# First adaLN scale by column halves with the first products between them, shift on TensorE, and 12 instead of 17 weight blocks split ahead, in a two-layer decoder trunk

## The chip, the cores and the metric

The kernel runs on one core of one Trainium2 chip. The metric is device time in microseconds (us) of one execution. The time before is 1517.57 us, the median of 3 runs (1512.85 to 1518.46). All rows below come from one profiled execution of it, which took 1515.52 us, with a span of 1513.8 us from the first to the last instruction.

Engines are written as the profile writes them: PE is TensorE, PEld its weight loads, DVE VectorE, ACT ScalarE, POOL GpSimd, SP SyncE, which issues most of the transfers.

## The reference

One sequence of 512 tokens of width 1024 goes through two layers. Each sub-layer is an RMS norm, an adaLN scale and shift computed from a condition vector `c`, a mixer, a gate and a residual add.

```
def ada_modulation(c, w, b):
    mod = jax.nn.silu(c) @ w + b
    return jnp.split(mod[:, None, :], 6, axis=-1)
...
    h = rms_norm(x, norm_mix) * (1 + sc_m) + sh_m
    fq, fk, fv, fgl, sq, sk, sv = _split(h @ w_in, EVEN_SPLITS)
...
    mix = jnp.concatenate([o_fox.reshape(B, S, -1), o_swa.reshape(B, S, -1)], axis=-1) @ w_out
    x = x + g_m * mix
    h = rms_norm(x, norm_ffn) * (1 + sc_f) + sh_f
    return x + g_f * swiglu(h, ffn_gate, ffn_up, ffn_down)
```

Layer 0 mixes with forgetting attention on half of the heads and sliding-window attention on the other half, then a dense SwiGLU of width 2816. Layer 1 mixes with sparse attention (an indexer picks 128 keys per query), then a top-2-of-8 expert SwiGLU and a final norm. Everything is float32 in and out.

## The kernel before

Activations stand transposed, features on the 128 partitions in 8 k-tiles (`KT`) of 512 tokens. A float32 product is made as three products of a high and a low half (`mm3`): weights high by activations high, high by low, low by high. The high half of a weight block is an ACT cast (`wh`), the low half a DVE subtraction (`wl`); raw blocks of 512 KB come over the SP queue into a pool of three buffers each (`weights(3, 3, 3)`). `norm` and the first stage make activations `h[k]` of the same two halves.

The work of one engine runs in one fixed order. A scheduler writes that order out when the program is built, by the order of the code and its own estimates; `tc.issue_after(x)` puts an instruction behind `x` in it. On the chip each engine takes its instructions strictly in this order and waits on semaphores.

The start works as follows. The norm sums (`ssqt`) are 16 small PE products; their root gives `rstd`, which PE spreads over the partitions, and DVE makes `xn[k]`, eight normed tiles without scale. Meanwhile `ada(0, 1, ...)` computes the first scale on PE: eight loads of 512 KB of `eada`, sixteen products with 32 output columns, four of which stand beside each other in the array at `tile_position` 0, 32, 64 and 96. Its sum is turned by four transposes (`ada_t`) and becomes `a` (name `A00`, in rows `A`). Then come `h[k]` of scale alone, and `NEARLY` = 3 first products of 24 matmuls each (`first`), on weight blocks that were split early (`early`). The shift is not in them yet: `ada_vector(0, (0,), ...)` computes it on DVE with 16 multiply-adds (`acc<-side`) and four PE products that sum over partitions (`ones`). It is added to the three finished products as a bias (`L844`, `L845`, `L850`), and to `h[k]` for all later products (`L859`, `L860`). The memory of this stage (`st_`) is reused by the attention stage (`at`), so the first instruction that writes there (`kd`, L608) waits until the last shifted `h[k]` is made.

In the dense SwiGLU PE makes gate and up products (`pj`) in two groups of 12 and 10 column blocks, each followed by `down` (`dn`). Beside them `ada_vector` computes later scales and shifts on DVE; its loads (`side`, two buffers) are issued by POOL when DVE has used up a buffer. The last of these chains is for the two vectors (1, (4, 5)). Also beside them, `split_ahead` prepares the input projection of layer 1 (`oin`, 17 blocks): load a block (`araw`), cast it (L316), subtract on DVE (L318), store the low half to DRAM (`olow`). Its steps are taken one in each of the eight steps of each `down`, and one in every second step of the second gate and up group. Layer 1 then loads raw and low halves of all 17 blocks (`wload`, L331).

In layer 1 POOL makes the two rope multiplications of each projection (`rope`, L568 and L569) while DVE picks keys (`choose`, MAX and MATCH_REPLACE); ACT casts the roped queries (`qs`), which the first scores (`ss`, L643) need.

## Time and profile before

| what | value |
|---|---|
| median of 3 runs | 1517.57 us |
| the profiled execution | 1515.52 us |
| its span | 1513.8 us |
| mean granted clock of PE | 0.979 |
| PE busy share of the span | 95% |
| DVE busy share | 68% |
| ACT busy share | 50% |
| POOL busy share | 9% |

The granted clock is 1.0 where PE has its full 2.4 GHz and 0.5 where it has 1.2 GHz. An idle time is noted in square brackets behind an instruction, with the instruction or transfer that ended it. Times are counted from the span's start.

### The profile page before, as it was taken

What the parts mean: (1) busy time and instruction counts of PE and PEld (TensorE: products, weight loads), DVE (VectorE), ACT (ScalarE), POOL (GpSimd) and SP (SyncE); (2) the same over time, 40 slices, a digit from 0 to 9 for tenths busy, and PEclk for the clock granted to TensorE, in tenths of its full rate; (3) what the DMA queues carried; (4) which work ended last, traced back from release to release, by engine and by line L of the source; (5) the groups of instructions that cost most, each with busy time, mean ns of one, the idle gap of its engine ahead of it and who ended that gap; (6) DMA issues with size and microseconds to landing.
All of it is one profiled execution on the core that took longest, in us unless ns stands there. A gap on an engine that the chain in (4) does not pass through costs nothing.

```text
span 1513.8 us, 23866 instructions
## 1 busy us (share of the span) xinstructions
PE 1431.5 (95%) x8683; PEld 1079.4 (71%) x8683; DVE 1033.3 (68%) x1909; ACT 750.6 (50%) x1257; POOL 129.9 (9%) x158
## 2 busy tenths in 40 slices
PE   5999999899999999898989999999999999999994
PEld 2766777678787878686767577776767777787773
DVE  5845587766665446644789753876767896897784
ACT  4554473332222332334436752755556675675672
POOL 1000000011010001001132100101010100100000
PEclk9999999899999999998999999999999999999997
DMA  8445325466688547644554102767787998897791
GB/s 315 141 128 148 82 83 191 170 209 210 196 261 292 169 130 260 230 148 123 169 156 127 48 29 86 301 220 243 254 267 250 319 342 262 276 377 247 268 388 60
DMA packets 91951, 309.32 MB, mean 204 GB/s; under 512 B 11304, under 2 KB 12088, under 8 KB 91824
## 3 DMA queue, kind: packets, MB, share of 16 engines
q1 hardware_dynamic: 77952, 259.93, 50.7%
q0 software_dynamic: 13872, 47.78, 10.3%
q8 instruction: 70, 1.15, 0.3%
q14 instruction: 57, 0.47, 0.1%
HBM read 278.64 MB, written 19.97 MB: 197 GB/s over the span
## 4 chain that ended last, share of the span: by engine, by line
PE 47%; DVE 5%; DMA 2%; ACT 2%; issue 1%; POOL 1%; SPq 0%; DVEq 0%; ACTq 0%; POOLq 0%
PE v L1370 4%; PE g L1363 3%; PE u L1364 3%; PE u L1363 3%; PE g L1365 3%; PE u L1365 3%; PE g L1364 3%; PE dn L336 2%; PE dn L338 2%; PE dn L337 2%; PE yv L1370 2%; PE yg L1363 2%; PE o L714 2%; PE ss L643 2%; PE yu L1363 1%; PE yu L1364 1%
## 5 line engine op out<-in xcount | busy, mean ns | idle before, releaser
L298 ACT CAST wh<-raw 128x1024 fp32r<-128x1024 f32 (+2 forms) x387 | 381.6, 992 | 406.8 <-PE dn L337 90.6
L299 DVE TENSOR_TENSOR wl<-raw,wh 128x1024 fp32r<-128x1024 f32 (+2 forms) x387 | 441.9, 1153 | 150.1 <-ACT wh L298 145.2
L336 PE MATMUL pj<-h,wh 128*128 128x512 f32 x560 | 226.1, 406 | 5.3 <-ACT h L486 3.2
L338 PE MATMUL pj<-h,wl 128*128 128x512 f32 (+1 forms) x560 | 225.0, 403 | 1.7 <-DVE wl L299 1.7
L337 PE MATMUL pj<-h,wh 128*128 128x512 f32 (+1 forms) x560 | 223.9, 401 | 0.1
L406 DVE SCALAR_TENSOR_TENSOR acc<-side,sc,acc 128x512 f32<-128x512 f32 x140 | 103.5, 750 | 52.9 <-DMA side<-in_oada 47.0
L336 PEld LDWEIGHTS pj<-h,wh 128*128 128x128 f32 x560 | 106.2, 190 | 36.7 <-ACT h L486 4.0
L338 PEld LDWEIGHTS pj<-h,wl 128*128 128x128 f32 (+1 forms) x560 | 106.4, 190 | 28.8 <-DVE wl L299 2.1
L337 PEld LDWEIGHTS pj<-h,wh 128*128 128x128 f32 (+1 forms) x560 | 105.9, 189 | 27.2 <-issue 2.2
L1363 PE MATMUL g<-wh,xe 128*128 128x512 f32 (+1 forms) x192 | 79.3, 413 | 1.2 <-ACT xe L1355 1.2
L338 PE MATMUL dn<-hid,wl 128*128 128x512 f32 x176 | 71.5, 406 | 2.3 <-DVE wl L299 2.3
L1363 PE MATMUL u<-wh,xe 128*128 128x512 f32 (+1 forms) x192 | 72.8, 379 | 0.0
L1364 PE MATMUL u<-wl,xe 128*128 128x512 f32 (+1 forms) x192 | 72.7, 378 | 0.0
L1365 PE MATMUL g<-wh,xe 128*128 128x512 f32 (+1 forms) x192 | 72.4, 377 | 0.0
L1364 PE MATMUL g<-wl,xe 128*128 128x512 f32 (+1 forms) x192 | 72.2, 376 | 0.0
L1365 PE MATMUL u<-wh,xe 128*128 128x512 f32 (+1 forms) x192 | 72.1, 376 | 0.0
L336 PE MATMUL dn<-hid,wh 128*128 128x512 f32 x176 | 71.3, 405 | 0.0
L337 PE MATMUL dn<-hid,wh 128*128 128x512 f32 x176 | 70.5, 401 | 0.0
L1370 PE MATMUL v<-raw,xf 128*32 128x128 f32 x1760 | 67.3, 276 | 0.0
L690 ACT ACTIVATE p<-p,st 128x128 f32<-128x128 f32 (+3 forms) x96 | 53.6, 560 | 25.0 <-DVE st L687 24.5
L1370 PEld LDWEIGHTS v<-raw,xf 128*32 128x32 f32 x1760 | 49.3, 109 | 21.4 <-issue 12.2
L526 DVE SCALAR_TENSOR_TENSOR xT<-dn,mod,xT 128x512 f32<-128x512 f32 x32 | 24.0, 750 | 53.1 <-PE dn L338 53.1
(419 smaller groups left out, 2661.2 us busy)
## 6 DMA issues: line engine op xcount, KB each, us to landing
raw<-in_xgu SPq DMA_DIRECT2D x128, 512.0 KB
raw<-in_xdn SPq DMA_DIRECT2D x88, 512.0 KB
side<-in_oada POOLq DMA_DIRECT2D x48, 512.0 KB, 4.7
raw<-in_xgu SPq DMA_DIRECT2D x64, 384.0 KB
raw<-in_egu SPq DMA_DIRECT2D x44, 512.0 KB
side<-in_eada SPq DMA_DIRECT2D x24, 512.0 KB
araw<-in_oin SPq DMA_DIRECT2D x16, 512.0 KB
olow<-araw SPq DMA_DIRECT2D x16, 512.0 KB
```

The source lines that it names most:

```text
L298: stream["cast"] = A.copy(wh[:, :n], raw[:, :n]).ins
L299: stream["sub"] = V.tensor_sub(wl[:, :n], raw[:, :n], wh[:, :n].bitcast(F32)).ins
L336: T.matmul(out_, wh, xh, start=start, stop=False)
L337: T.matmul(out_, wh, xl, start=False, stop=False)
L338: T.matmul(out_, wl, xh, start=False, stop=stop)
L406: V.scalar_tensor_tensor(s, r, sc[:, k:k + 1], s, op0=ALU.mult, op1=ALU.add)
L643: T.matmul(b[:, j, :nk], qs[p, a, t * P:(t + 1) * P], k[p, c, :nk], start=a == c, stop=a == 1, tile_position=(64 * j, 0))
L690: A.activation(ps_[j][:, :nk], ps_[j][:, :nk], AF.Exp, bias=st[:, j:j + 1], scale=-1.0, accum_out=rc[:, i, j:j + 1])
L1363: T.matmul(o, x[0], wh, start=first, stop=False)
L1364: T.matmul(o, x[0], wl, start=False, stop=False)
L1365: T.matmul(o, x[1], wh, start=False, stop=last)
L1370: T.matmul(o[32 * j:32 * j + 32], x[2], w[:, j * width:(j + 1) * width], start=first, stop=last, tile_position=(0, 32 * j), skip_group_che ...
```

## The change

There are two independent parts.

The first is the start. The scale is computed in two halves of its columns (`scale(0)`, `scale(1)`): each half has four loads and eight products, two rounds of four beside each other in the array. The loads of the first half go ahead of the early weight blocks. After the first half of the scale, k-tiles 0 to 3 of `h` are made, and the first four k-tiles of products 0 and 1; then the second half of the scale, the first four k-tiles of product 2, and the last four k-tiles of all three. The shift is no longer computed on DVE: `ada(0, 0, ...)` makes it with sixteen products, eight behind product 0 and eight behind product 1. The loads of later weight blocks are kept behind the loads of this stage (`pin`).

The second part is `AHEAD = 12`: only 12 of the 17 blocks of `oin` are split ahead, and only in the steps of `down`. The other five are split when they are used, with the subtraction on POOL.

```
+AHEAD = 12
...
-        self.ap, self.at, self.low = ap, 0, None
+        self.ap, self.at, self.low, self.left = ap, 0, None, 0
...
-        stream["load"] = nc.sync.dma_start(raw[:, :n], src).ins
+        with tc.issue_after(stream["pin"]) if stream.get("pin") else ExitStack():
+            stream["load"] = nc.sync.dma_start(raw[:, :n], src).ins
...
-        stream["sub"] = V.tensor_sub(wl[:, :n], raw[:, :n], wh[:, :n].bitcast(F32)).ins
+        stream["sub"] = (G if blocks.low else V).tensor_sub(wl[:, :n], raw[:, :n], wh[:, :n].bitcast(F32)).ins
...
     def wload(blocks, nk, ncol):
-        if blocks.low is not None:
+        if blocks.low and blocks.left:
+            blocks.left -= 1
...
+            def scale(g, after=None):
+                raws = [load(src(g, kp), 1024) for kp in range(4)]
+                yield
+                pt = bank("pt", "ada")
+                with tc.issue_after(after) if after else ExitStack():
+                    for k in range(KT):
+                        q = 32 * (k % 4)
+                        T.matmul(pt[q:q + 32, :], cb[:, k], raws[k // 2][:, k % 2 * 512:k % 2 * 512 + 512], start=k < 4,
+                                 stop=k > 3, tile_position=(0, q))
+                rows_ = t512("ada_row")
+                A.copy(rows_, pt)
+                pc = aux("ada_t")
+                for n in range(4):
+                    T.transpose(pc[:, n * P:(n + 1) * P], rows_[:, n * P:(n + 1) * P], identf)
+                part = t512("ada_s")[:, :4]
+                V.tensor_reduce(part, pc.rearrange("p (n h r) -> p n h r", n=4, r=32)[:, :, :, 0], axis=AX.X, op=ALU.add)
+                c = slice(4 * g, 4 * g + 4)
...
+                for k in range(4 * g, 4 * g + 4):
+                    hk = hp.tile([P, 2, S], F32R, name=f"h{k}", tag=f"h{k}")
+                    A.activation(hk[:, 0], xn[k], AF.Copy, scale=a[:, k:k + 1])
+                    V.scalar_tensor_tensor(hk[:, 1], xn[k], a[:, k:k + 1], hk[:, 0].bitcast(F32), op0=ALU.mult, op1=ALU.subtract)
+                    h.append(hk)
+                yield
...
-            fill(ada(0, 1, load, "pt"), 99)
...
+            fill(scale(0), 2)
+            for i in range(NEARLY):
+                early(i)
+            begin(0, range(4))
+            second = scale(1, begin(1, range(4)))
+            fill(second, 1)
+            shift = ada(0, 0, load, "mm")
+            fill(second, 1)
+            begin(2, range(4))
             for i in range(NEARLY):
-                if i == SHIFT:
-                    fill(ada_vector(0, (0,), st_, nc.sync, NS0), 99)
...
+                ins = begin(i, range(4, KT))
+                if i < NEARLY - 1:
+                    with tc.issue_after(ins):
+                        fill(shift, 2)
+            stream["pin"] = stream["early"]
+            fill(shift, 1)
...
-                            [KT * n if n <= P else KT // 2 * n for n in O_IN for _ in range(1 if n <= P else 2)])
+                            [KT * n if n <= P else KT // 2 * n for n in O_IN for _ in range(1 if n <= P else 2)][:AHEAD])
...
-                if grp == FFN_GROUPS[-1] and c % 2:
-                    fill(ahead)
...
-            oin.low = Blocks(olow)
+            oin.low, oin.left = Blocks(olow), AHEAD
```

`begin(i, ks)` makes product `i` for the k-tiles `ks` with `mm3`.

The order of the instructions shows three places. The first is PE at the very start, before and then of the changed kernel; `ada` are the products of the scale, `ssqt` the norm sums, `rstd` the spreading of the root, `first` the first products.

```order
L461 MATMUL ssqt<-ones_102,ssqa 128x1 x4
L461 MATMUL ssqt<-ones_102,sq 128x1 x4
L382 MATMUL ada<-st,cb 32x512
L475 MATMUL rstd<-identf,rs_r 128x128 x4
L382 MATMUL ada<-st,cb 32x512 x15
L360 MATMUL ada_t<-identf,ada_row 128x128 x4
L336 MATMUL first<-h_253,early_193 128x512 x3
```

```order
L828 MATMUL ada<-st,cb 32x512
L464 MATMUL ssqt<-ones_102,ssqa 128x1 x4
L464 MATMUL ssqt<-ones_102,sq 128x1 x4
L828 MATMUL ada<-st,cb 32x512 x7
L478 MATMUL rstd<-identf,rs_r 128x128 x4
L834 MATMUL ada_t<-identf,ada_row 128x128 x4
L339 MATMUL first<-h_224,early_193 128x512 x2
```

Before, one of the sixteen products of the scale stood ahead of `rstd`; now all eight of the first half do, one of them ahead of the norm sums.

On DVE at the same place, `xn` are the normed tiles, `early` the low halves of the three early weight blocks, `A` the scale; the rows run from the root to the first low halves of `h`, without the first seven of the eight `xn`.

```order
L812 TENSOR_TENSOR early_194<-st,early_193 128x8x128
L796 TENSOR_TENSOR xn_191<-xT,rstd 128x512
L369 TENSOR_REDUCE ada_s<-ada_t 128x8
L370 TENSOR_TENSOR mod_243<-ada_s,vec 128x8
L819 SCALAR_TENSOR_TENSOR A_251<-mod_243,vec 128x8
L812 TENSOR_TENSOR early_194<-st,early_193 128x8x128
L824 SCALAR_TENSOR_TENSOR h_253<-xn_177,A_251,h_253 128x512
```

```order
L799 TENSOR_TENSOR xn_191<-xT,rstd 128x512
L836 TENSOR_REDUCE ada_s<-ada_t 128x4
L815 TENSOR_TENSOR early_194<-st,early_193 128x8x128
L838 TENSOR_TENSOR ada_s<-ada_s,vec 128x4
L815 TENSOR_TENSOR early_194<-st,early_193 128x8x128
L839 SCALAR_TENSOR_TENSOR A_195<-ada_s,vec 128x4
L815 TENSOR_TENSOR early_194<-st,early_193 128x8x128
L843 SCALAR_TENSOR_TENSOR h_224<-xn_177,A_195,h_224 128x512
```

The scale still stands behind all eight `xn`, and two of the three subtractions for the early blocks, which stood ahead of `xn`, now stand between the reduction and the scale.

The second place is DVE in the second gate and up group, in the chain of (1, (4, 5)): `acc` are its multiply-adds, `araw` is the subtraction of the split ahead, `sg` and `hid` belong to the gate.

```order
L404 TENSOR_SCALAR acc<-side,sc 128x512
L406 SCALAR_TENSOR_TENSOR acc<-side,sc,acc 128x512 x3
L299 TENSOR_TENSOR wl<-raw,wh 128x1024
L406 SCALAR_TENSOR_TENSOR acc<-side,sc,acc 128x512
L318 TENSOR_TENSOR araw<-araw,awh 128x1024
L406 SCALAR_TENSOR_TENSOR acc<-side,sc,acc 128x512 x3
L973 TENSOR_TENSOR sg<-pj,sg 128x512
```

```order
L407 TENSOR_SCALAR acc<-side,sc 128x512
L409 SCALAR_TENSOR_TENSOR acc<-side,sc,acc 128x512 x3
L301 TENSOR_TENSOR wl<-raw,wh 128x1024
L409 SCALAR_TENSOR_TENSOR acc<-side,sc,acc 128x512 x4
L1010 TENSOR_TENSOR sg<-pj,sg 128x512
```

The subtraction is gone from between the multiply-adds, at two places of this chain; the order of the rest is the same there.

The third place is POOL in the sparse attention: pairs of rope multiplications, and in the changed kernel the subtractions of the late blocks (`wl`).

```order
L568 TENSOR_TENSOR rq<-rq,cosT 128x512
L569 TENSOR_TENSOR rr<-rr,sinT 128x512
L568 TENSOR_TENSOR rq<-rq,cosT 128x512
L569 TENSOR_TENSOR rr<-rr,sinT 128x512
L568 TENSOR_TENSOR rq<-rq,cosT 128x512
L569 TENSOR_TENSOR rr<-rr,sinT 128x512
```

```order
L571 TENSOR_TENSOR rq<-rq,cosT 128x512
L572 TENSOR_TENSOR rr<-rr,sinT 128x512
L301 TENSOR_TENSOR wl<-raw,wh 128x1024
L571 TENSOR_TENSOR rq<-rq,cosT 128x512
L572 TENSOR_TENSOR rr<-rr,sinT 128x512
L301 TENSOR_TENSOR wl<-raw,wh 128x1024
L571 TENSOR_TENSOR rq<-rq,cosT 128x512
L572 TENSOR_TENSOR rr<-rr,sinT 128x512
```

The three pairs are those of the first key block, the second key block and the first query block; a subtraction now stands ahead of the second pair and ahead of the third.

## Rows read from the trace of the kernel before

**Rows 1.** The page: busy us, share of the span and instructions of each engine.
```profile
PE 1431.5 (95%) x8683; PEld 1079.4 (71%) x8683; DVE 1033.3 (68%) x1909; ACT 750.6 (50%) x1257; POOL 129.9 (9%) x158
```

**Rows 2.** Timeline of the start: start us, us, engine, line, operation, tiles [idle before].
```profile
15.59 1.85 PE L461 MATMUL ssqt<-ones,sq 128*128 128x1 f32 x8
19.80 1.08 PE L475 MATMUL rstd<-identf,rs_r 128*128 128x128 f32 x4 [0.52 <-DVE rs_r L441]
20.92 4.87 DVE L796 TENSOR_TENSOR xn<-xT,rstd 128x512 f32<-128x512 f32 x8
27.79 1.05 PE L382 MATMUL ada<-st,cb 128*32 128x512 f32 x4 [0.24 <-DMA st<-in_eada]
30.68 0.17 DVE L819 SCALAR_TENSOR_TENSOR A<-mod,vec 128x8 f32<-128x8 f32 x1
30.77 1.22 DVE L812 TENSOR_TENSOR early<-st,early 128x1024 fp32r<-128x1024 f32 x1
31.66 0.96 PE L336 MATMUL first<-h,early 128*128 128x512 f32 x3 [1.42 <-ACT h L823]
31.91 5.38 DVE L824 SCALAR_TENSOR_TENSOR h<-xn,A,h 128x512 fp32r<-128x512 f32 x8
```

**Rows 3.** Weight loads of the scale's products on PE, one row for four products.
```profile
21.67 0.20 PEld L382 LDWEIGHTS ada<-st,cb 128*32 128x32 f32 x4 [0.66 <-issue]
22.52 0.20 PEld L382 LDWEIGHTS ada<-st,cb 128*32 128x32 f32 x4 [0.66 <-issue]
```

**Rows 4.** Timeline of the end of the start.
```profile
51.80 0.17 DVE L370 TENSOR_TENSOR mod<-ada_t,vec 128x8 f32<-128x8 f32 x1 [1.39 <-PE ada_t L360]
52.59 0.33 PE L844 MATMUL bias<-early,b 128*2 128x384 f32 x1 [0.82 <-DVE b L841]
60.45 0.68 ACT L608 ACTIVATE kd<-first,bias 64x512 fp32r<-64x512 f32 x1 [3.33 <-DVE h L860]
63.99 0.39 PE L508 MATMUL pt<-wh,h 128*128 128x256 f32 x1 [1.88 <-ACT vt L615]
```

**Rows 5.** Stretches: us, busy (instructions) per engine, granted clock of PE, DMA share, GB/s.
```profile
61.00:64.50 3.50, 1.62 (x14) 1.42 (x13) 3.26 (x6) 3.17 (x7) 0.00 (x0) 1.00 0.36 75
64.60:68.00 3.40, 3.40 (x19) 3.40 (x18) 3.24 (x7) 0.68 (x1) 0.00 (x0) 0.50 0.72 155
624.40:631.10 6.70, 5.67 (x16) 4.60 (x17) 1.58 (x5) 1.61 (x4) 0.00 (x0) 0.50 0.71 243
631.20:638.00 6.80, 6.80 (x31) 5.49 (x30) 3.54 (x4) 2.45 (x4) 0.00 (x0) 1.00 0.49 152
```

**Rows 6.** Timeline of PE at the start of the second down product.
```profile
625.43 1.11 PE L360 MATMUL ada_t<-identf,ada_row 128*128 128x128 f32 x4 [3.88 <-ACT ada_row L357]
```

**Rows 7.** Timeline of DVE and SP in the last chain of the dense SwiGLU.
```profile
586.35 1.22 DVE L318 TENSOR_TENSOR araw<-araw,awh 128x1024 fp32r<-128x1024 f32 x1
591.95 0.42 SPq L311 DMA_DIRECT2D araw<-in_oin  x1
601.59 1.54 DVE L406 SCALAR_TENSOR_TENSOR acc<-side,sc,acc 128x512 f32<-128x512 f32 x2 [4.09 <-DMA side<-in_oada]
614.95 0.75 DVE L406 SCALAR_TENSOR_TENSOR acc<-side,sc,acc 128x512 f32<-128x512 f32 x1 [2.33 <-DMA side<-in_oada]
616.75 2.32 DVE L406 SCALAR_TENSOR_TENSOR acc<-side,sc,acc 128x512 f32<-128x512 f32 x3
623.56 0.68 DVE L973 TENSOR_TENSOR sg<-pj,sg 128x512 f32<-128x512 f32 x1
```

**Rows 8.** Timeline of POOL, DVE and PE before the first sparse scores.
```profile
772.80 1.30 POOL L568 TENSOR_TENSOR rq<-rq,cosT 128x512 f32<-128x512 f32 x1 [8.87 <-DVE m L1029]
776.57 1.72 POOL L569 TENSOR_TENSOR rr<-rr,sinT 128x512 f32<-128x512 f32 x1
780.19 0.68 DVE L570 TENSOR_TENSOR rq<-rq,rr 128x512 f32<-128x512 f32 x1
781.58 0.80 PE L643 MATMUL ss<-kd,qs 64*128 64x256 f32 x4 [1.73 <-ACT qs L595]
```

More of the change, by code (lines that the diff above doesn't have):

```diff
@@ L337, in mm3 @@
         T.matmul(out_, wh, xl, start=False, stop=False)
-        T.matmul(out_, wl, xh, start=False, stop=stop)
+        return T.matmul(out_, wl, xh, start=False, stop=stop)
     sc = cst.tile([P, KT], F32, name="sc")
@@ L800, in load @@
                 t = st_.tile([P, n], F32, tag="st", name="st", bufs=7)
-                nc.sync.dma_start(t, src)
+                stream["early"] = nc.sync.dma_start(t, src).ins
                 return t
@@ L812, in early @@
                 V.tensor_sub(wl[:, :, c], raw, wh[:, :, c].bitcast(F32))
-            for i in range(FIRST):
-                early(i)
-            fill(ada(0, 1, load, "pt"), 99)
-            for i in range(FIRST, NEARLY):
-                early(i)
-            a = cst.tile([P, KT], F32, name="A00")
-            V.scalar_tensor_tensor(a, mods[0, 1], 1.0, vec[:, V_NORM:V_NORM + 8], op0=ALU.add, op1=ALU.mult)
-            h = []
-            for k in range(KT):
-                hk = hp.tile([P, 2, S], F32R, name=f"h{k}", tag=f"h{k}")
-                A.activation(hk[:, 0], xn[k], AF.Copy, scale=a[:, k:k + 1])
-                V.scalar_tensor_tensor(hk[:, 1], xn[k], a[:, k:k + 1], hk[:, 0].bitcast(F32), op0=ALU.mult, op1=ALU.subtract)
-                h.append(hk)
@@ L826, in build @@
-            first = []
-            for i in range(NEARLY):
-                if i == SHIFT:
-                    fill(ada_vector(0, (0,), st_, nc.sync, NS0), 99)
-                c = slice(i * P, (i + 1) * P)
-                o = bank(("pt", "o", "pt")[i], "first")
-                for k in range(KT):
-                    mm3(o, wh[:, k, c], wl[:, k, c], h[k][:, 0], h[k][:, 1], k == 0, k == KT - 1)
-                first.append(o)
-            if SHIFT == 3:
-                fill(ada_vector(0, (0,), st_, nc.sync, NS0), 99)
+            src = ada_blocks(0, 1)
@@ new lines, in build @@
+            a = cst.tile([P, KT], F32, name="A00")
+            h = []
+            def scale(g, after=None):
[15 more added lines that the diff above has]
+                c = slice(4 * g, 4 * g + 4)
+                V.tensor_add(part, part, vec[:, V_ADA + 8 + 4 * g:V_ADA + 12 + 4 * g])
+                V.scalar_tensor_tensor(a[:, c], part, 1.0, vec[:, V_NORM + 4 * g:V_NORM + 4 * g + 4], op0=ALU.add, op1=ALU.mult)
+                for k in range(4 * g, 4 * g + 4):
[4 more added lines that the diff above has]
+                yield
@@ new lines, in build, with begin @@
+            first = []
+            def begin(i, ks):
+                c = slice(i * P, (i + 1) * P)
+                if len(first) == i:
+                    first.append(bank(("pt", "o", "pt")[i], "first"))
+                for k in ks:
+                    ins = mm3(first[i], wh[:, k, c], wl[:, k, c], h[k][:, 0], h[k][:, 1], k == 0, k == KT - 1)
+                return ins.ins
+            fill(scale(0), 2)
+            for i in range(NEARLY):
+                early(i)
+            begin(0, range(4))
@@ L930, in build @@
                 fill(later, NA)
+            stream["pin"] = None
             kd = k_dup(at, rope(at, project(ein, h), bufs=2), bufs=3)
```

## The prediction

> **What bounds the kernel now.** I read the page first: PE is busy 95% of the span [rows 1], so a gain must come from PE's idle time, from its clock, or from work taken off it. Then the timeline of the start, where PE is not yet full, and the timelines at PE's long idle times. In the start the reader is to see two chains. The scale waits for the last of eight loads, whose products stand at 27.79; `A` is ready at 30.85, the first product starts at 31.66, and the low halves of `h`, which pace it, at 31.91 [rows 2]. At the other end the shift is ready at 51.97 and the bias products start at 52.59; `kd` starts at 60.45, when DVE has made the last shifted `h`, and PE waits 1.88 us for a copy behind it, until 63.99 [rows 4].
>
> A wait costs twice. After that 1.88 us the granted clock is 0.50 for 3.4 us, though PE is busy; after a wait of 3.88 us at 625.43 [rows 6] it is 0.50 for 6.7 us, with 16 instructions recorded against 31 in as long a stretch at 1.00 [rows 5]. So these cost some 1.7 and 3.4 us on top.
>
> **Part 1, the start.** The change wants products on half of the scale while the other half is loaded. What decides is when `A` comes. Norm sums end at 17.44 [rows 2]. One product of the scale now stands ahead of them, seven behind, and `rstd` behind those; before, `rstd` started at 19.80. Rows of four of these products start 0.85 us apart [rows 3], which is 512 columns at 1.2 GHz, and each product takes two such passes. Two rounds of four are four passes, 3.4 us, and they end at 20.9; the one ahead of the norm sums may push them by 0 to 1 us, I take 0.5: 21.4. `xn` starts 1.12 us after `rstd` starts (20.92 against 19.80), so at 22.5, and its eight instructions take 4.87: 27.4. Then in DVE's order two subtractions of 1.22 and three small instructions of 0.17 stand up to `A`, 2.9 us: 30.3. A third subtraction follows, so the first low half of `h` starts at 31.5 against 31.91. The first products, which were to gain from four loads instead of eight, come 0.4 us earlier: the load was not the only thing late, the normed tiles are late next.
>
> From there to the shift, PE gets more work. Added: 1.7 us for the second half of the scale (four passes at full clock, half of 0.85 each), 3.4 us for the sixteen products of the shift, 0.5 us of transposes; removed: the four products that summed DVE's shift, about 2 us by the same pass. The second half of the scale (sum, copy, transposes, `h`) lies beside the first k-tiles of product 2, all but about 0.5 us of it. DVE loses 16 multiply-adds, but PE was the later of the two there, so that is worth nothing except that the two scalings of `xn` that stood beside the end are done before: -0.5. Sum: -0.4 + 3.6 + 0.5 - 0.5, rounded +3 for the shift at full clock. The load of the last shift block waits for a buffer that the first shift products free; it has some 3 us beside product 1, about what a load needs, so I count nothing for it and keep 1 us in the bound. The later weight blocks now come behind all these loads; their casts and subtractions stand among the shift's last steps on ACT and DVE, but the products of the last k-tiles cover them.
>
> Then the clock. By the times above PE has nothing from about 23.5 (its transposes of the half scale, behind `rstd`) to 30.5, seven us, longer than either wait of [rows 4, 6]. So the products start at 0.50 and run so for 3.4 to 6.8 us, as after those waits [rows 5]: 1.7 to 3.4 us lost. I take 2, since the first few are paced by DVE: the shift 5 us later. The DVE chain behind it (block subtraction, eight low halves) is the one of before without the scalings, about 0.8 shorter: `kd` some 4.2 us later, at 64.6. Behind `kd` ACT has the value copies that PE waited for, so PE goes on at 68.2 instead of 63.99. But PE reaches that point later too and waits under 1 us, so the 1.7 us of slow clock there go. Part 1 is then +4.2 - 1.7 = **+2.5**. Bounds: at full clock the shift comes 3 and `kd` 2.2 later, +0.5 without the slow stretch at 64, and -1 if all the terms of half a us fall the other way; slow for the longest time, and a slow stretch at 64 as before, +5.
>
> **Part 2, the dense SwiGLU.** Five loads, casts, subtractions and stores go from the second gate and up group. PE is full there, so all of that is hidden and worth nothing, but for one chain that ends late: the multiply-adds of (1, (4, 5)). The last three stand at 616.75 to 619.07; the gate's `sg` comes late by them and ends at 624.24; ACT's copy of `ada_row`, in order behind that, ends PE's wait at 625.43, 3.88 us long [rows 6, 7]. Two subtractions of the split ahead stand between the multiply-adds (586.35 is one): 1.2 us each [rows 7]. The waits of 4.09 and 2.33 us for `side` follow loads of `araw` (591.95 is the first) and their stores; without that traffic I take half of them off, 3.2 us. In all 5.6 against 3.9 that are needed. So the wait goes, and with it 6.7 us at half clock: -3.9 - 3.3 = **-7.2**. Bounds: 0, if the chain is as late as before; -8, if it frees something behind it too. What would be late next is PE itself.
>
> **Part 3, the sparse attention.** Each of five low halves is now a subtraction of 128x1024 on POOL, in order with the rope. The trace has POOL at 1.30 to 1.72 us for 128x512 [rows 8]; doubled, 2.6 to 3.4, I take 3.0. DVE does 128x1024 in 1.22 [rows 2], which bounds it from below. Here a rule speaks for a smaller price: the Trainium skill, GPSIMD Engine Reference, section 3.1, has a two-input add at about twice VectorE's time; by it a subtraction would be an estimated 2.4 us, and the sum 0.6 lower. The rope rows agree with the ratio or lie above it: 1.30 and more against 0.61 for `xn` of that shape [rows 2].
>
> Two of the five matter. The first stands ahead of the second key block's rope, which waited 8.87 us for something else until 772.80 [rows 8]: hidden. The second stands ahead of the first query block's rope, which ended at 778.29. Its addition on DVE started at 780.19, so 1.9 us are free and 1.1 are not. Queued behind the addition are the cast of `qs` and the first scores, for which PE already waits 1.73 at 781.58 [rows 8]. So **+1**. The other three stand ahead of ropes that are wanted later. Bounds: -1.5 (five low halves fewer on the SP queue, past which the rope's exchanges are issued) and +4 (each of the two at 3.4, none hidden, less the 1.9, or a later block that POOL holds back while PE still uses its buffer).
>
> **The sum.** 2.5 - 7.2 + 1 = -3.7. Against the profiled execution's 1515.5 that is 1511.8; the median of the runs shown is 2.0 above that execution, which gives 1513.9. I forecast **1513**.
>
> **The rivals.**
> - The start keeps its clock. For it: between 28.84 (27.79 and 1.05) and 31.66 PE has little in the trace of before and runs on at full speed. Against it: the new gap is over twice as long. Part 1 is then near 0, in all -6.2 to -7: 1509.
> - The change does not do what it says in part 2: the wait at 625.43 stays. For it: the chain starts when PE lets go of the sums of the chain before, which the change does not move, and most of its loads had no split traffic beside them. Then 1515.5 + 2.5 + 1 = 1519.
> - POOL becomes the engine that sets the sparse attention. Its place is the subtraction ahead of a rope: it waits until PE has used up the buffer three blocks before, and the rope queued behind it waits too, then DVE's addition, ACT's cast and PE's scores. Each such wait costs PE its length and up to 3.4 us of slow clock. From about two waits of 3 us on it eats part 2: 2 x 3 + 3.4 = 9.4, in all 1515.5 + 2.5 - 7.2 + 9.4 = 1520.2, slower than before. Against it: only one of the five is on the path by the rows.
>
> **How the numbers follow.** A difference under 0.5%, 7.6 us, is one that a measurement of this kernel can hardly tell from none. My forecast has 0.46, with a range of its own from 1508 to 1517; the clock kept at the start 0.20; the wait that stays 0.18; POOL 0.16. Faster than 1510.0: most of the second case and a quarter of the forecast, 0.27. Slower than 1525.2: nearly half of the POOL case and a little of the wait that stays, 0.08. The rest, 0.65, is the same. The range takes in the first three cases and half of the fourth: 1506 to 1521.
>
> **What would show it.** In the profile of the changed kernel: `A` of the first half at about 30, not at 25; a granted clock of 0.50 in the first products; the shift at 56 to 57; `kd` near 64.6, and under 1 us of waiting at the value products, without a slow stretch after it. At 620 no wait of PE for `ada_row` over 0.5 us and a clock of 1.00. Before the first sparse scores a wait of PE about 1 us longer than 1.73. I am wrong if `A` comes before `xn` is done, if PE still waits at the second down product, or if PE waits for `qs` or low halves by more than 3 us in the sparse attention.

## The result: slower by 0.57%, and the profile after

The changed kernel took 1522.23 us (median of 20 runs, 1513.56 to 1526.71), the kernel before 1514.11 us (20 runs on the same chip, 1506.04 to 1519.07). The ratio is 1.0057, with a 95% interval of 1.0041 to 1.0072: some 8.6 us slower. The forecast was 1513, with a range from 1506 to 1521. Of the experiments below, one execution of the new start alone took 2762.72 us, which its ratio leaves out and its median of 1511.74 counts.

The two profiled executions differ by 10.7 us of span. I cut both at PE instructions that they share: the first product of the first `down` of the SwiGLU, the spread of `rstd` in layer 1, and the first expert product (`g`).

| stretch | before, us | after, us | difference | forecast |
|---|---|---|---|---|
| to the SwiGLU's first `down` (434.0 and 438.3) | 434.0 | 438.3 | +4.3 | +2.5 |
| from there to `rstd` of layer 1 (687.5 and 684.0) | 253.5 | 245.6 | -7.8 | -7.2 |
| from there to the first expert product (955.2 and 965.6) | 267.8 | 281.6 | +13.9 | +1 |
| from there to the end | 558.6 | 558.9 | +0.3 | 0 |

The forecast fails most in one stretch, the sparse attention. The stretches of that part, first of the kernel before (columns as in [rows 5]: us, busy time of PE, PEld, DVE, ACT and POOL with instructions, granted clock of PE, DMA share, GB/s):

```profile
687.47:748.90 61.43, 55.97 (x297) 40.77 (x297) 37.81 (x61) 28.75 (x53) 14.22 (x10) 0.93 0.39 116
748.90:829.50 80.60, 76.74 (x372) 56.43 (x370) 75.34 (x215) 38.97 (x94) 20.91 (x16) 0.96 0.53 159
829.50:895.05 65.55, 61.39 (x448) 38.91 (x447) 48.10 (x157) 48.41 (x150) 9.88 (x15) 1.00 0.12 37
```

and of the changed kernel, cut at the same instructions:

```profile
683.96:750.26 66.30, 58.07 (x296) 42.07 (x297) 38.13 (x62) 28.74 (x53) 13.34 (x10) 0.90 0.36 106
750.26:838.35 88.09, 78.83 (x372) 57.05 (x370) 80.15 (x215) 40.69 (x95) 35.64 (x22) 0.94 0.44 123
838.35:905.49 67.14, 62.72 (x447) 39.57 (x447) 49.41 (x156) 47.20 (x148) 6.13 (x15) 0.97 0.10 29
```

The second line is where the late blocks are. DVE runs the same 215 instructions and needs 80.15 us for them, not 75.34. The timeline of the changed kernel there shows why:

```profile
775.28 2.41 POOL L301 TENSOR_TENSOR wl<-raw,wh 128x1024 fp32r<-128x1024 f32 x1
776.33 1.92 DVE L573 TENSOR_TENSOR rq<-rq,rr 128x512 f32<-128x512 f32 x1
783.63 0.79 PE L646 MATMUL ss<-kd,qs 64*128 64x256 f32 x4 [2.71 <-ACT qs L598]
796.56 2.37 POOL L301 TENSOR_TENSOR wl<-raw,wh 128x1024 fp32r<-128x1024 f32 x1 [7.11 <-ACT wh L300]
797.03 2.44 DVE L599 TENSOR_TENSOR qs<-rq,qs 128x512 fp32r<-128x512 f32 x1 [0.45 <-ACT qs L598]
799.53 0.38 PE L646 MATMUL ss<-kd,qs 64*128 64x256 f32 x2 [1.46 <-DVE qs L599]
810.59 2.40 POOL L301 TENSOR_TENSOR wl<-raw,wh 128x1024 fp32r<-128x1024 f32 x1 [4.21 <-ACT wh L300]
811.07 2.47 DVE L599 TENSOR_TENSOR qs<-rq,qs 128x512 fp32r<-128x512 f32 x1 [0.20 <-ACT qs L598]
814.53 0.62 PE L646 MATMUL ss<-kd,qs 64*128 64x256 f32 x6 [1.09 <-DVE st L690]
838.35 0.62 PE L646 MATMUL ss<-kd,qs 64*128 64x256 f32 x6 [1.74 <-DVE st L690]
845.82 0.44 PE L646 MATMUL ss<-kd,qs 64*128 64x384 f32 x2 [1.56 <-DVE st L690]
```

A subtraction on POOL takes 2.4 us. The DVE instructions of L573 and L599 read two tiles each: the rope's addition, and the subtraction that makes the low half of a query block (`qs`). Such an instruction on 128x512 takes 0.68 us when nothing is beside it (the addition in [rows 8]). The one that starts at 797.03, beside POOL's subtraction, takes 2.44. It ends just behind it: 796.56 + 2.37 = 798.93, and the last 0.5 us lie behind that. PE waits for what comes of it. The Trainium skill, SBUF — State Buffer, section "SBUF: two separate sides", states this: VectorE and GpSimd share a port pair that one of them holds for a whole instruction, also against a VectorE instruction with two SBUF inputs when the GpSimd instruction reads SBUF. The trace agrees, and the forecast had left it out. By the same trace the picks beside it keep their length: a MAX8 of 128x384 at 775.85 takes 0.56 us, as one that has no subtraction beside it.

### The profile page after: what moved, and what is told of

Read it like the earlier page. It is cut to its first block, busy times and chain, and to the rows that moved or that the text cites. A ratio compares the mean times of both kernels' runs of the same rounds, so it can differ in the third digit from the quotient of the medians.

```text
span 1524.5 us, 23910 instructions
## 1 busy us (share of the span) xinstructions
PE 1434.7 (94%) x8715; PEld 1081.8 (71%) x8715; DVE 1024.3 (67%) x1892; ACT 748.3 (49%) x1253; POOL 139.7 (9%) x163
## 4 chain that ended last, share of the span: by engine, by line
PE 45%; DVE 7%; DMA 2%; ACT 2%; issue 2%; POOL 1%; SPq 0%; DVEq 0%; ACTq 0%; POOLq 0%
PE v L1405 4%; PE g L1398 3%; PE u L1399 2%; PE u L1398 2%; PE g L1400 2%; PE g L1399 2%; PE u L1400 2%; PE dn L339 2%; PE dn L340 2%; PE dn L341 2%; PE yv L1405 2%; PE yg L1398 2%; PE o L717 2%; PE yg L1399 1%; PE yu L1398 1%
## 5 line engine op out<-in xcount | busy, mean ns | idle before, releaser
L300 ACT CAST wh<-raw 128x1024 fp32r<-128x1024 f32 (+2 forms) x392 | 386.8, 993 | 417.2 <-issue 102.4
L409 DVE SCALAR_TENSOR_TENSOR acc<-side,sc,acc 128x512 f32<-128x512 f32 x126 | 94.0, 750 | 49.7 <-DMA side<-in_oada 44.9
L339 PE MATMUL dn<-hid,wh 128*128 128x512 f32 x176 | 69.6, 396 | 0.0
L340 PE MATMUL dn<-hid,wh 128*128 128x512 f32 x176 | 69.1, 393 | 0.0
```

Source lines behind the costliest of these rows:

```text
L300: stream["cast"] = A.copy(wh[:, :n], raw[:, :n]).ins
L339: T.matmul(out_, wh, xh, start=start, stop=False)
L340: T.matmul(out_, wh, xl, start=False, stop=False)
L409: V.scalar_tensor_tensor(s, r, sc[:, k:k + 1], s, op0=ALU.mult, op1=ALU.add)
```

## The experiments

Ratios are against runs of the kernel before on the same chip; a us figure is the ratio less 1 times 1512. "The stretch" is from `rstd` of layer 1 to the first expert product, in the one profiled execution of each kernel (267.8 before, 281.6 after). The stretch has a spread of its own: six kernels that add nothing to POOL and keep the old order there have 266.2 to 271.2. And one execution need not be a typical one: the profiled one of all but the start is the fastest of its twelve, that of the five added subtractions the slowest, that of the six fills the fastest.

### The parts, each alone

**The low halves subtracted on VectorE again.**

```
-        stream["sub"] = (G if blocks.low else V).tensor_sub(...)
+        stream["sub"] = V.tensor_sub(...)
```

> The changed kernel with the five late low halves subtracted on VectorE instead of POOL, all else as changed. In the changed kernel the stretch from the sparse attention's norm to the first expert product is 281.6 us against 267.8 before, and POOL's 2.4 us subtractions lie beside additions of VectorE that take 2.44 instead of 0.68. Theory A (a subtraction on POOL holds up VectorE's two-input instructions beside it): these long additions go, five subtractions of 1.22 come onto VectorE, the stretch falls to 272 to 277, the total by 5 to 9 us, to 1513 to 1517. Theory B (what costs is that these five blocks are split here at all, cast and load and buffer order, on whichever engine): the stretch stays within 2 us of 281.6, the total near 1522. Theory C (part of the loss, the 4.9 us ahead of the key blocks, lies where no subtraction stands on POOL and is its own): those 4.9 us stay whatever happens behind them.

Measured: 1523.51, ratio 1.0064 (1.0040 to 1.0088); stretch 281.9. No gain. The DVE instructions of 2.4 us are gone, but another wait has come, in PE's timeline:

```profile
832.85 0.79 PE L341 MATMUL pj<-h,wl 128*128 128x512 f32 x1 [4.82 <-DVE wl L301]
843.05 0.62 PE L646 MATMUL ss<-kd,qs 64*128 64x256 f32 x6 [3.07 <-DVE st L690]
```

DVE is nearly full there (80.71 of the 87 us from 751 on), and a low half in its order comes late. The number is the one of theory B, but it doesn't show that the engine is all the same: the two kernels wait for different things, and this one has another order again, in which some 45 of DVE's instructions stand elsewhere.

**The new start alone** (the kernel before with the start of the changed one).

> The kernel before with the new start alone: half scale first, first products by halves, shift by quarter-array products; the split ahead and the sparse attention as before. From the trace of the changed kernel the start is worth +3.2 us at the first softmax scores and +4.4 us by the first down product. Theory A: that is a steady price, total +3 to +5 us over before (1517 to 1519). Theory B: the 1.2 us behind the first scores (half clock after the same wait of 3.1 us) are chance, and the start costs what the prediction had, +2.5 (1516.5). Rival: it is worth nothing or gains, then what the profile shows at 100 us is given back later.

Measured: 1511.74, ratio 0.9991 (0.9973 to 1.0008), that is -4.1 to +1.2 us. That is the rival of the expectation: the start is not what made the kernel slower.

**All but the start** (the changed kernel with the old start).

> The changed kernel with the old start: twelve blocks split ahead, none of it in the second gate and up group, the last five split in the sparse attention with the subtraction on POOL. From the two traces: -7.9 us in the dense SwiGLU, +13.9 in the sparse attention. Theory A: both are steady, total +4 to +7 us over before (1518 to 1521). Theory B (the sparse attention's loss is a chance of when POOL and VectorE meet, and depends on what comes before it): with another arrival time it differs by several us in the stretch from the norm to the first expert product, 270 to 278 instead of 281.6, and the total is at or under that of before.

Measured: 1518.74, ratio 1.0048 (1.0021 to 1.0075), +7.3 us; stretch 277.8. Theory A: the loss is here.

**All seventeen blocks ahead, none in the second gate and up group.**

```
-                if grp == FFN_GROUPS[-1] and c % 2:
-                    fill(ahead)
...
-            fill(aside)
+            fill(aside, 1 if last else 2)
```

> The kernel before (old start, all seventeen blocks split ahead), but no step of the split in the second gate and up group: the first down product takes two steps per column block instead of one. It should have the gain of the dense SwiGLU without any subtraction on POOL. Theory A (the gain comes from taking the split out of the second gate and up group): PE waits under 2 us for the last modulation's row and the clock stays at 1.00 there, total 5 to 8 us under before (1506 to 1509). Theory B (the gain needs the five blocks gone altogether): the chain of multiply-adds is late again, or the first down product waits for its own low halves, total within 2 us of before.

Measured: 1520.60, ratio 1.0048 (1.0022 to 1.0074); stretch 267.7. Both theories missed the total, +7.3 us. The last modulation is hardly late (a wait of 0.80 us), but the first `down` of the SwiGLU now waits for its own low halves, as theory B had it; two of such rows of PE:

```profile
462.66 0.50 PE L338 MATMUL dn<-hid,wl 128*128 128x512 f32 x1 [1.76 <-DVE wl L299]
474.68 0.50 PE L338 MATMUL dn<-hid,wl 128*128 128x512 f32 x1 [1.51 <-DVE wl L299]
```

This trace is of an execution 7.6 us under the median, so it doesn't show where all of the +7.3 comes from.

**The dense part alone** (twelve blocks ahead; the last five low halves are loaded from five other blocks, so the right ones are left out).

> The dense SwiGLU's part of the change alone: the old start, twelve blocks split ahead and none of it in the second gate and up group. The last five blocks load low halves in the sparse attention as before (those of five other blocks, so that part of the output is left out), so nothing is added there. Theory A (my step of -7.2 holds): total 5 to 8 us under before, 1505 to 1507 on 1512.4; PE waits under 1.6 us for the last modulation's row. Theory B (the chain of multiply-adds is paced by the landings of its own loads, which the change does not touch: 16.2 and 19.1 us of such waits in two profiles without the split, 17.6 and 18.8 in two with it): only the 2.4 us of two subtractions go, the wait comes and goes with the execution, total 0 to 4 us under before, 1508.5 to 1512.5.

Measured: 1506.74, ratio 0.9966 (0.9942 to 0.9989), -5.1 us; stretch 266.2. That is the near end of theory A, with an interval (-8.8 to -1.7) that reaches into B. So the sparse part of the change costs 7.3 + 5.1 = 12.4 us, give or take 5 by the two intervals.

### What the sparse part's 12.4 us are

**A subtraction on POOL that nobody needs** (the kernel before; the other engines keep their order instruction for instruction).

```
             A.copy(wh[:, :n], raw[:, :n])
+            blocks.left -= 1
+            if blocks.left < 0:
+                G.tensor_sub(raw[:, :n], raw[:, :n], wh[:, :n].bitcast(F32))
```

> The kernel before, all seventeen blocks split ahead, with one subtraction of 128x1024 on POOL added behind the cast of each of the last five blocks in the sparse attention (onto a buffer that is done with, so nothing waits for its result but the buffer's next load). Theory A (a two-input instruction of VectorE stands still while POOL subtracts): additions of VectorE of 1.9 to 2.5 us where they took 0.68, PE waits behind them, the stretch from the sparse attention's norm to the first expert product 275 to 280 us against 267.8, total +6 to +11 us. Theory B (what costs is that low halves come late, or the schedule around them): nothing waits for these, the stretch stays within 2 us of 267.8, total within 2 us of before.

Measured: 1515.75, ratio 1.0019 (1.0002 to 1.0037), +2.9 us; stretch 276.5. The stretch is the one of theory A, the total is less than half of its least.

**Fills in its place** (`for _ in range(3): G.memset(raw[:, :n], 0.0)`).

> The same as the kernel with five subtractions added, but each is replaced by three fills of 128x1024 with zero on POOL, at the same places of its order and of about the same length (a fill of 128x512 takes 0.53 us in the start, so three of 128x1024 some 2.7 to 3.2), and reading nothing. Theory A1 (POOL's reading is what stops VectorE): VectorE's additions stay at 0.68, the stretch stays within 2 us of 267.8. Theory A2 (any instruction on POOL stops them): as long as in the kernel with subtractions. Theory C (in-order POOL: the rope behind the added work comes late, VectorE is not slowed): the stretch grows by about as much as with subtractions, 275 to 280, with VectorE's additions at 0.68 and idle time ahead of them.

Measured: 1515.52, ratio 1.0025 (1.0008 to 1.0042), +3.8 us; stretch 267.3, as in theory A1. The same DVE instruction (the low half of the same query block), first beside a subtraction:

```profile
801.51 2.39 POOL L333 TENSOR_TENSOR raw<-raw,wh 128x1024 f32<-128x1024 f32 x1 [7.55 <-ACT wh L330]
802.09 2.37 DVE L599 TENSOR_TENSOR qs<-rq,qs 128x512 fp32r<-128x512 f32 x1
```

and beside fills:

```profile
796.08 2.98 POOL L334 MEMSET raw<- 128x1024 f32 x3 [8.28 <-ACT wh L330]
796.69 0.68 DVE L600 TENSOR_TENSOR qs<-rq,qs 128x512 fp32r<-128x512 f32 x1
```

That settles the mechanism for this kind: POOL's reading stops DVE's two-input instruction, POOL's being busy does not. It doesn't settle the price, since the totals of the two are alike.

**Twice the dose of each** (two subtractions; six fills).

> The kernel before with two subtractions on POOL behind the cast of each of the last five blocks, ten in all, onto buffers that are done with. The five alone gave +2.9 us in the total and 276.5 against 267.8 us in the stretch from the norm to the first expert product, in one execution. Theory A (each is worth what it stops of VectorE, about 1.2 to 1.8 us where it meets an addition): the double gives +6 to +12 us in the total, a stretch of 276 to 285, and additions of VectorE up to 4.5 us long. Theory B (the +2.9 is the distance between two kernels by chance): total within 3 us of before.

> The kernel before with six fills of 128x1024 on POOL (0.96 us each, 5.9 together) behind the cast of each of the last five blocks. Three each gave +3.8 us in the total with no addition of VectorE over 1.1 us and a stretch of 267.3. Theory A1 (POOL's length ahead of a rope counts, in order, though VectorE is not stopped): additions of VectorE stay at 0.68 and start late, the stretch is 273 to 282, total +7 to +13 us. Theory A2 (fills are hidden and the +3.8 of three each came from elsewhere): total within 4 us of before, stretch within 3 of 267.8.

Measured: subtractions 1519.66, ratio 1.0045 (1.0023 to 1.0067), stretch 277.6; fills 1519.14, ratio 1.0039 (1.0015 to 1.0063), stretch 272.3. The longest DVE instruction of this kind is 2.8 us, not 4.5. Ten subtractions cost 6.8 us against 2.9 for five; the two intervals overlap, and the stretch is only 1.1 us longer, so that more of them cost more is likely and not shown. In the stretch subtractions cost more than fills, by 9.2 us with five and 5.3 with ten; in the totals (+6.8 and +5.9) they don't. What the fills cost in the total stays open: in their trace of three each the stretch is as short as before.

**The dense part and the five dead subtractions.**

> The dense SwiGLU's part alone (old start, twelve blocks ahead, none in the second gate and up group, low halves of the last five blocks still loaded, from five other blocks), with the five subtractions on POOL added onto buffers that are done with. PE, VectorE and ScalarE keep the order of the kernel with the dense part alone, POOL does what it does in the changed kernel. It differs from the changed kernel with the old start (+7.2 us) in two things only: the products don't need what POOL makes, and the order that the scheduler gives PE, VectorE and ScalarE in the sparse attention is the old one. The dense part alone gave -5.2, the five subtractions alone +2.9. Theory A (POOL's subtractions make the loss by themselves): total +4 to +8 us over before, as the changed kernel with the old start. Theory B (most of the loss is the order that follows from low halves made late): total -4 to 0 us.

Measured: 1513.71, ratio 1.0001 (0.9979 to 1.0023), +0.2 us; stretch 274.3. Just outside theory B, and far from A. Against the dense part alone that is +5.3 us, and the order is the same on PE, DVE and ACT. The stretch in the dense part alone, and with the subtractions:

```profile
676.20:942.40 266.20, 249.59 (x1414) 181.20 (x1414) 189.79 (x510) 136.61 (x326) 47.70 (x47) 0.98 0.35 112
```

```profile
680.60:954.90 274.30, 253.50 (x1415) 183.13 (x1415) 197.11 (x510) 136.94 (x326) 60.66 (x52) 0.96 0.34 108
```

The same 510 instructions in the same order keep DVE busy for 7.3 us more: that is about the time that it stood still beside the subtractions.

**The order of the changed kernel without the subtractions** (all but the start; low halves filled with zero, 0.96 us each).

> The changed kernel with the old start, but the low halves of the last five blocks are filled with zero on POOL (0.96 us each, reading nothing) instead of subtracted (2.4 us): that part of the product is left out. PE, VectorE, ScalarE, POOL and SP stand in the order of the changed kernel with the old start but for some ten instructions. That kernel gave 1.0048, the dense part alone 0.9966, the dense part with dead subtractions in the old order 1.0001. Theory A (the order costs by itself): 0.9995 to 1.0030, a stretch from the norm to the first expert product of 272 to 277 us, with waits of PE for the row maxima of VectorE at its end as in the changed kernel. Theory B (the rest was the subtractions too): 0.9955 to 0.9985, a stretch of 266 to 270.

Measured: 1511.96, ratio 1.0005 (0.9984 to 1.0026), +0.8 us; stretch 274.1. Theory A. When the low halves are made late, the scheduler writes another order in the query blocks (some 50 of PE's 1414 instructions stand elsewhere), and this kernel takes 5.9 us more than the dense part alone. No projection of PE waits 0.3 us or more for a low half here; PE waits 2.03 and 1.02 us for row maxima of DVE at the end of the scores, as the changed kernel does (1.74 and 1.56 above).

Part of this is the same stop, at other places. The stretch, and one of the places:

```profile
680.60:954.70 274.10, 255.05 (x1415) 184.41 (x1415) 194.79 (x510) 137.12 (x326) 50.57 (x52) 0.96 0.32 99
833.22 1.32 POOL L572 TENSOR_TENSOR rr<-rr,sinT 128x512 f32<-128x512 f32 x1
833.34 1.75 DVE L573 TENSOR_TENSOR rq<-rq,rr 128x512 f32<-128x512 f32 x1
835.84 0.79 PE L646 MATMUL ss<-kd,qs 64*128 64x384 f32 x6 [1.02 <-DVE st L690]
```

DVE's 510 instructions take 5.0 us more than in the dense part alone (194.79 against 189.79), and nothing on POOL reads here but the rope. In the new order more of DVE's instructions start beside a rope multiplication: this addition takes 1.75 us instead of 0.68, and PE's wait of 1.02 us for the row maximum right behind it is as long as that loss. How much of the 5.9 us in the total is this, and how much is the order itself, the five fills or the five loads of low halves that this kernel does not make, is not shown.

**Fourteen blocks ahead** (`AHEAD = 14`, three late blocks; PE is back in its old order).

> The changed kernel with the old start and fourteen blocks split ahead instead of twelve, as many as the sixteen column blocks of the two down products have steps for: three late blocks subtracted on POOL instead of five. With three, the scheduler leaves PE in the order of the kernel before. Theory A (the order that follows from five late blocks costs some 5 to 7 us by itself, a subtraction on POOL about 1): total -5.2 + 3 = -2, from -4 to +1 us over before, a stretch from the norm to the first expert product of 268 to 273. Theory B (a late low half costs some 2.5 us each, by whatever way): -5.2 + 3 x 2.5, +1 to +4 us, a stretch of 273 to 276.

Measured: 1510.79, ratio 0.9993 (0.9972 to 1.0015), -1.1 us; stretch 270.2. Theory A in both figures, though the interval of the total (-4.2 to +2.3) reaches into theory B, and 270.2 lies in the spread of kernels without any subtraction.

The four corners, us against before:

| | old order | new order |
|---|---|---|
| no subtraction on POOL | -5.1 | +0.8 |
| five subtractions on POOL | +0.2 | +7.3 |

Each of the two costs 5 to 7 us, and they add up. Each difference has an uncertainty of some 5 us, so each is barely clear of none; the four agree with the four stretches (266.2, 274.1, 274.3, 277.8) in sign, and less than fully in size.

### A faster version

**Three buffers for the loads of the modulations** (the kernel before).

```
-    ... ada_vector(l, w, fp, G, 2, ended[-1]) ...
+    ... ada_vector(l, w, fp, G, 3, ended[-1]) ...
```

> The kernel before with three buffers instead of two for the loads of the modulations' weights in the dense SwiGLU, and nothing else changed. Theory B of the dense SwiGLU (the chain of multiply-adds is paced by the landings of its loads): the waits for them in the second gate and up group fall from 17.6 us to under 9, the chain ends before PE wants it, the wait of 3.88 us and the half clock behind it go, total 3 to 7 us under before. Theory A (the split's work in VectorE's order is what makes it late): the chain stays late by the 2.4 us of subtractions and the wait stays above 1 us, total within 2 us of before.

Measured: 1502.86, ratio 0.9928 (0.9912 to 0.9944), -10.9 us: theory B, and more than it had. DVE's waits for these loads in the second gate and up group are 10.9 us in all, not 17.6. The transposes that came at 625.43 behind a wait of 3.88 [rows 6] follow without one:

```profile
617.10 0.60 PE L360 MATMUL ada_t<-identf,ada_row 128*128 128x128 f32 x4
```

This beats both kernels, by more than the 7.2 us that I had given to the wait and its slow clock. In the traces 6.8 us lie behind the start of the second `down` (60.6 against 67.4 us to `rstd`), and 4.2 in the first `down`, where a wait of 2.02 us for a low half and 3.4 us of half clock are gone; but that wait differs between executions of kernels that are alike there, so what the third buffer has to do with it is open.

**With the new start as well.**

> The kernel before with the new start and with three buffers for the loads of the modulations' weights in the dense SwiGLU: the two parts that the runs so far show as harmless or better, and without the split change. The third buffer alone gave 0.9928 (-10.9 us), the new start alone 0.9991. Theory A (the new start is free in the total): 1500 to 1504 on 1512. Theory B (the start costs the 3 us that the traces show by the first softmax scores): 1504 to 1507.

Measured: 1501.43, ratio 0.9930 (0.9901 to 0.9959), -10.6 us. Theory A, and no gain from the start.

## Why the prediction was wrong, point by point

**Part 1, the start (+2.5): the steps were right, the price in the total is not borne out.** The changed kernel's start:

```profile
29.73 0.16 DVE L839 SCALAR_TENSOR_TENSOR A<-ada_s,vec 128x4 f32<-128x4 f32 x1
30.69 1.22 PE L339 MATMUL first<-h,early 128*128 128x512 f32 x2 [7.48 <-ACT h L842]
30.94 2.73 DVE L843 SCALAR_TENSOR_TENSOR h<-xn,A,h 128x512 fp32r<-128x512 f32 x4
57.48 0.17 DVE L373 TENSOR_TENSOR mod<-ada_s,vec 128x8 f32<-128x8 f32 x1
64.11 0.68 ACT L611 ACTIVATE kd<-first,bias 64x512 fp32r<-64x512 f32 x1 [1.32 <-DVE bias L889]
68.65 0.38 PE L511 MATMUL pt<-wh,h 128*128 128x256 f32 x1 [0.44 <-ACT vt L618]
```

and its clock:

```profile
25.20:35.40 10.20, 4.71 (x11) 3.39 (x12) 9.26 (x16) 4.05 (x7) 0.56 (x1) 0.51 0.72 231
```

`A` at 29.73 (forecast 30.3), low halves of `h` at 30.94 (31.5), the shift at 57.48 (56 to 57), `kd` at 64.11 (64.6), a wait of 0.44 us (under 1). PE idled 7.48 us, and 4.7 us of the first products ran at half clock (3.4 to 6.8). The first softmax scores come at 94.0 to 94.2 in three executions with the new start and at 97.6 in the fourth; in twelve with the old start at 90.6 to 93.0. So 2 us are lost there. The totals don't show them: -1.4 us alone, with an interval that ends at +1.2, under the forecast +2.5; +0.3 beside the third buffer, and +1.4 between the changed kernel and the one with the old start (1.0057 and 1.0048). Where they come back is open. One figure of the working was wrong without harm: 512 columns at 1.2 GHz are 0.43 us; the 0.85 that the sum uses is what [rows 3] show.

**Part 2, the dense SwiGLU (-7.2): right in kind.** It measured -5.1, and the -7.2 lies within the interval (-8.8 to -1.7). In the changed kernel DVE's chain still waits for `side`, and the gate's `sg` follows directly behind it:

```profile
615.23 2.32 DVE L409 SCALAR_TENSOR_TENSOR acc<-side,sc,acc 128x512 f32<-128x512 f32 x3 [3.35 <-DMA side<-in_oada]
618.26 0.68 DVE L1010 TENSOR_TENSOR sg<-pj,sg 128x512 f32<-128x512 f32 x1
624.70 0.44 PE L363 MATMUL ada_t<-identf,ada_row 128*128 128x128 f32 x2 [1.51 <-ACT ada_row L360]
```

and the stretch behind it (columns as in [rows 5]):

```profile
624.70:631.50 6.80, 6.80 (x32) 5.67 (x33) 2.96 (x7) 2.27 (x3) 0.00 (x0) 1.00 0.74 224
```

The wait of 3.88 is 1.51, and the clock behind it 1.00, not 0.50 [rows 5]. The `sg` behind the multiply-adds starts at 618.26, against 618.99 in the kernel before, and ACT's copy of `ada_row` starts 5.8 us behind it in both; PE is done with its last products 1.6 us later than before. So against PE the chain came some 2.4 us earlier in this trace, not the 5.6 of the forecast. The `sg` at 623.56 that the forecast read as the late one is the next one; between the two stand other instructions, a subtraction of the split in the `down` among them, which the change leaves there. But the wait doesn't go in each execution. In the eight kernels without the split in that group it was 3.91, 2.18, 1.51, 1.10, 0.80 and three times none; in the six with it, and with two buffers, 3.88 to 3.91 each time. The waits for `side` there were 15.5 us in the mean against 19.4, so the 3.2 us that I took off for the absent traffic were about right. The forecast had the term as if it held always, and with that it was probably too large.

**Part 3, the sparse attention (+1, bounds -1.5 to +4): the step that failed.** It put: "Two of the five matter", and priced a subtraction by its place in POOL's order ahead of a rope. The size of that term was hit: the wait at 781.58 of 1.73 us [rows 8] became 2.71. But that is luck, for POOL's place in the order was not what ended last there:

```profile
779.33 1.76 POOL L572 TENSOR_TENSOR rr<-rr,sinT 128x512 f32<-128x512 f32 x1
779.29 2.35 DVE L609 TENSOR_TENSOR kd<-rq,kd 64x512 fp32r<-64x512 f32 x2
782.25 0.68 DVE L573 TENSOR_TENSOR rq<-rq,rr 128x512 f32<-128x512 f32 x1
```

The rope ended on POOL at 781.09, and DVE's addition came 1.2 us later, behind DVE's own work: the addition at 776.33 had taken 1.92 us beside the subtraction (0.88 in the kernel before), and of the two low halves `kd` one stood still beside the rope (2.35 us for both, 1.38 before). POOL's own time was even priced too high, 3.0 us where the profile has 2.40. The Trainium skill, GPSIMD Engine Reference, section 3.1, by whose rule I had an estimated 2.4, is borne out. What was missing are two terms, neither of them in the bounds. A subtraction stops a two-input instruction of DVE wherever the two meet, also where no rope waits, in a stretch where DVE is full (75.34 of 80.60 us busy before): 5.3 us by the totals. And the order: I read it only at the places of my terms, and took the moved products of the query blocks to be worth nothing; 5.9 us, in part by the same stop beside the rope. Together the part measured 12.4 us, give or take 5, against +1.

**The rivals.** The third came nearest: POOL, 1520.2, slower. Its mechanism was another: POOL waiting for buffers and holding back ropes. In the changed kernel's trace the subtractions that had to wait on POOL waited for ACT's cast, not for a buffer, and no wait of PE of 0.3 us or more was for a low half made on POOL. So that the number 1520.2 came near is luck too. Its price had been looked for on POOL alone.

## What to carry to other kernels

When work moves to POOL, its price is not only POOL's time and place: count DVE's two-input instructions that lie beside it, and ask whether DVE has slack to stand still. When the producer of an operand moves to a slower engine, compare the order of all engines over the whole stage, not only at the moved instruction, and look at what the new order puts beside POOL. For a chain that waits for its loads try one more buffer before taking other work away: here that gave 10.9 us against 5.1.

## What else the runs showed of the hardware

The stop needs no subtraction. In thirteen of sixteen traces the rope multiplications of the indexer's first query block follow those of its key block on POOL without a gap, and an addition of 64x512 on DVE beside them takes 3.0 us. In the changed kernel (a second multiplication follows on POOL from 708.02 to 709.30, and the addition ends at 709.84):

```profile
705.53 1.28 POOL L572 TENSOR_TENSOR rr<-rr,sinT 64x512 f32<-64x512 f32 x1
706.78 1.27 POOL L571 TENSOR_TENSOR rq<-rq,cosT 128x512 f32<-128x512 f32 x1
706.84 3.00 DVE L573 TENSOR_TENSOR rq<-rq,rr 64x512 f32<-64x512 f32 x1 [11.08 <-POOL rr L572]
```

In the other three, the kernel before among them, a transfer lands later, POOL has a gap of 0.4 to 0.5 us, and the addition gets in:

```profile
709.98 0.68 DVE L570 TENSOR_TENSOR rq<-rq,rr 64x512 f32<-64x512 f32 x1 [10.51 <-POOL rr L569]
710.48 1.34 POOL L568 TENSOR_TENSOR rq<-rq,cosT 128x512 f32<-128x512 f32 x1 [0.54 <-DMA rr<-rq]
```

So the one trace that the forecast was read from did not show the stop at this place; most executions would have. It did show it elsewhere, and in both directions:

```profile
834.64 1.22 DVE L299 TENSOR_TENSOR wl<-raw,wh 128x1024 fp32r<-128x1024 f32 x1
834.83 2.16 POOL L568 TENSOR_TENSOR rq<-rq,cosT 128x512 f32<-128x512 f32 x1 [1.51 <-DVE st L687]
835.87 2.20 DVE L299 TENSOR_TENSOR wl<-raw,wh 128x1024 fp32r<-128x1024 f32 x1
836.95 2.25 POOL L569 TENSOR_TENSOR rr<-rr,sinT 128x512 f32<-128x512 f32 x1
```

The two engines take turns here. POOL's multiplication, 1.30 us long in [rows 8], takes 2.16 and ends about 1.1 us behind the first DVE subtraction (835.86); the second subtraction takes 2.20 instead of 1.22 and ends 1.1 us behind that multiplication (836.99); and so on. The missing term could have been read from this trace.

Two-input instructions are not the only ones. A DVE copy of 128x256 (`rcb<-rc`), 0.28 us long elsewhere, takes 1.11 at 807.75 in the kernel before, beside a rope multiplication, and 0.53 and 0.66 beside fills in the kernel with six of them.

The same wait is not followed by the same clock. PE waited 3.15 us for a row maximum before the score product at 100.20 in the kernel before and ran on at 1.00; in the changed kernel it waited 3.14 us at 103.38 and a stretch of 3.4 us at 0.50 followed. Over the sixteen traces this wait is 2.9 to 3.6 us long; behind it come 6.8 us at 0.50 in nine of them, 3.4 us in five and none in two, one of which is the kernel before. One trace of each is not enough to price a slow stretch.
